# A two-layer hybrid block on one Trainium2 core: the heads' mean squares on GpSimd instead of TensorE

## The chip, the cores and the metric

The kernel runs on one core of one Trainium2 chip. The metric is the device time of one execution in microseconds (us). It was run three times: 1317.89 us in the median, 1317.74 to 1318.26. TensorE is PE in the profile (its weight loads are PEld), VectorE is DVE, ScalarE is ACT, GpSimd is POOL, SyncE is SP.

## What is computed

A sequence of 16 meta tokens and 256 tokens of width 1024 (272 columns in the kernel) passes through two layers. Each layer has a mixer of three branches (retention with 4 heads of 256 values, HGRN2 with 8 heads of 128, differential attention with 8 heads of 128) and a convolved feed-forward part. Each head's output is normalised by its own root mean square:

```python
def _rms(x):
    xf = x.astype(F32)
    return xf * lax.rsqrt(jnp.mean(xf * xf, axis=-1, keepdims=True) + EPS)
...
    o = _rms(from_chunks(o)) * jax.nn.silu(gate)        # retention
...
    o = _rms(from_chunks(o)) * jax.nn.silu(gate)        # hgrn2
...
    o = _rms(o) * subln_g.astype(F32) * (1.0 - lambda_init)   # differential attention
```

The change touches only this mean over a head's features, `jnp.mean(xf * xf, axis=-1)`.

## The kernel before

**Layout.** Activations stand transposed: features across the 128 partitions, tokens along the columns. A head of 128 features is one tile of 128 partitions by 272 columns (258 in the last layer, where only what the output needs is computed; 256, 242 or 128 in attention, whose leading and trailing tokens are treated apart). So the mean over a head's features is a sum across partitions, for each column.

**The main stream.** Every weight matrix is cut into tiles of 128 by 128, and eight tiles make a chunk of 512 KB that SP loads into `wraw` (3 buffers). ACT rounds it into `whi`, DVE subtracts to get `wlo` (4 buffers each), and PE makes three products for each tile, high by high, high by low and low by high (lines 905 to 907, in `products`). That is 11,862 products with all the small ones.

**The heads.** Between the main products PE runs the small products of the heads. `ret_head` (line 1015, four calls a layer) takes two PSUM banks of the tag `acc` for its two halves of 128 values, squares both with ACT, adds them with DVE, and multiplies both halves by the inverse root. `hg_outputs` (line 1210, two calls a layer, "a" and "b", four heads each) and `da_head` (line 1263, eight calls a layer, through `sub_norm`, line 1319) take one `acc` bank a head; `da_tail` (line 1327, two calls a layer) calls `sub_norm` once for its 128 left-over columns. The tag `acc` has two banks, so a later head's first product waits until an earlier head's `tt(y, o, r)` has read its bank. All in all there are 22 means a layer, 44 in the kernel.

**One mean** is `mean`, line 958: ACT rounds the squares into `hsh`, DVE subtracts to get `hsl`, and PE multiplies both by a matrix of 1/128 (`ones_h`) into a bank `ms`, which then holds the mean in every partition. `rsqrt` (line 804) makes two ACT passes of it, Ln with `eps` and Exp, into `hr`.

**GpSimd** has little to do: the adds and products of the layer norms (`y`, `sum`), and small copies and clears for the heads (`tails`, `wts`, `dt`, `da`, `am`, `near`, `at`).

**Order.** No engine's order is written out by hand. Each instruction is registered with a key (a due time, from a clock that counts main products) and a cost, and `_Plan.order` (line 447) simulates all five engines with those costs and deals out each engine's instructions in the order in which they would start. On the chip each engine then runs its list in that order and waits where an operand isn't ready. The costs are in `_Engine` (line 558). A changed cost or dependency anywhere can move any instruction after it.

**Memory.** The tag `slot` has 13 buffers (`SLOTS`) of 128 partitions by 1088 columns, 4352 bytes of each partition, for the blocks of the mixer. `_places` (line 142) puts the weights at chosen offsets, counted in lines of 256 bytes, against the activations that they meet.

Of the kernel before, what the change touches and what calls it, by code (L numbers as in the profile page):

```python
# [10 lines left out]

F32 = mybir.dt.float32
F32R = mybir.dt.float32r
U8 = mybir.dt.uint8
AF = mybir.ActivationFunctionType
ALU = mybir.AluOpType
PSUM = bass.MemoryType.PSUM
ADD, SUB, MUL = ALU.add, ALU.subtract, ALU.mult

P = 128  # L20
# [3 lines left out]
T = META + SEQ  # L24
# [10 lines left out]
TAIL = T - 2 * P  # L35
BANK = 512
CHUNK_TILES = 8
SLOTS = 13
LEAD = 6.0
MARGIN = 12.0  # L40
EARLY = 12.0
# [516 lines left out]
class _Engine:  # L558
# [5 lines left out]
    def __getattr__(self, method):  # L564
        f = getattr(self.engine, method)

        def call(*args, **kw):
            aps = [(k, x) for k, x in list(enumerate(args)) + list(kw.items()) if isinstance(x, bass.AP)]
            outs = [x for k, x in aps if k in (0, "out", "accum_out")]
            ins = [x for k, x in aps if k not in (0, "out", "accum_out")]  # L570
            n = math.prod(outs[0].shape[1:])
            cost = self.fixed + self.each * n
            if self.name == "act":
                cost += 0.093 * (len(aps) - 2) - (0.043 if ins[0].tensor.name in self.plan.psum else 0.0)
            elif self.name == "pool" and method != "memset":
                cost += 1.6e-3 * n
            if method == "reciprocal":
                cost += 7 * self.each * n
            elif method == "tensor_tensor_scan":
                cost += self.each * n  # L580
            elif method == "transpose":
                cost = 0.11
            elif method == "matmul" and args[1].dtype == F32R:
                cost = max(0.107, n / 2400 + 0.003)
            elif method == "matmul":
                cost = max(0.214 if args[1].shape[-1] > 32 else 0.07, 4 * n / 2400)
            elif method == "dma_start":
                cost = self.fixed + self.each * n * outs[0].shape[0]
            self.plan.add(self.name, lambda: f(*args, **kw), cost, outs, ins, args[2] if method == "activation" else None)  # L589

        return call
# [57 lines left out]
def _trace(ctx, tc, plan, a, depth, probe):  # L649
    nc = tc.nc  # L650
    act = _Engine(plan, nc.scalar, "act", 0.094, 0.833e-3)
    dve = _Engine(plan, nc.vector, "dve", 0.068, 1.042e-3)
    pe = _Engine(plan, nc.tensor, "pe", 0.0, 4 / 2400)
    pool = _Engine(plan, nc.gpsimd, "pool", 0.04, 0.85e-3)
# [7 lines left out]
    tp = ctx.enter_context(tc.tile_pool(name="tp", bufs=2))  # L662
# [6 lines left out]
    def new(pool_, shape, dt, tag, bufs, name):  # L669
        serial[0] += 1  # L670
        return plan.tile(pool_, shape, dt, tag, bufs, f"{name}_{serial[0]}")

    def fixed(shape, name, dt=F32):
        return new(cp, shape, dt, name, 1, name)

    def slot(name, dt=F32):
        return new(sp, [P, 4 * T], dt, "slot", SLOTS, name)

# [12 lines left out]
    def bank(name):  # L691
        return new(bp, [P, 512], F32, "bank", 2, name)
# [46 lines left out]
        pool.memset(t, value)  # L739
        return t  # L740

    def ones_round(value, name):
        t = fixed([P, P], name, F32R)
        f = slot("ones")[:, :P]
        pool.memset(f, value)
        act.activation(t, f, AF.Copy)
        return t

    ones_d = ones(1.0 / D, "ones_d")

    plan.key = -9.5
# [1 line left out]
    for _ in range(WARM):  # L753
        pe.matmul(warm[:, :P], ones_d, ones_d, start=True, stop=True)
    plan.key = -5.0
    ones_h = ones_round(1.0 / 128, "ones_h")
    eps = fixed([P, 1], "eps")
    pool.memset(eps, EPS)
    fmap = fixed([P, DEPTH], "fmap")
# [44 lines left out]
    def rsqrt(out, ms, scale=1.0):  # L804

        act.activation(out, ms, AF.Ln, bias=eps, scale=scale)
        act.activation(out, out, AF.Exp, scale=-0.5)

    class Norm:
# [29 lines left out]
        def mean(self):  # L839

            tt(self.acc[:, 0, :], self.acc[:, 0, :], self.acc[:, 1, :], ADD)
            self.ps = bank("ms")[:, self.first : T]
            pe.matmul(self.ps, ones_d, self.acc[:, 0, :], start=True, stop=self.rest is None)
# [111 lines left out]
        act.activation(vs, pm[:, :P], AF.Copy)  # L955
        return vs

    def mean(ones_, sq):

        n = sq.shape[1]  # L960
        hi = new(tp, [P, T], F32R, "hsh", 2, "hsh")[:, :n]
        lo = new(tp, [P, T], F32R, "hsl", 1, "hsl")[:, :n]
        act.activation(hi, sq, AF.Copy)
        dve.tensor_tensor(out=lo, in0=sq, in1=hi.bitcast(F32), op=SUB)
        ms = bank("ms")[:, :n]
        pe.matmul(ms, ones_, hi, start=True, stop=False)
        pe.matmul(ms, ones_, lo, start=False, stop=True)
        return ms

    def split_blocks(name, blocks, t0):  # L970

# [8 lines left out]
    for li in range(depth):  # L980
# [4 lines left out]
        t0 = T0 if last else 0  # L985
# [29 lines left out]
        def ret_head(hd):  # L1015
            q, k, vt, gate = st["rq"], st["rk"], st["rvt"], st["rg"]
            if hd == 0:
                st["dec"] = slot4("dec")
                sync.dma_start(st["dec"].rearrange("p h t -> p (h t)"), a["dec"])
            dec = st["dec"][:, hd, :]  # L1020

            s1 = bank("s1")
            a1 = temp(T + P + TAIL, "wts")
            parts = ((0, t0, t0, dec[:, t0:]), (P, P, T, dec[:, : P + TAIL]))
            for k0, q0, at, _ in parts:
                pe.matmul(s1[:, at : at + T - q0], k[:, hd, k0 : k0 + P], q[:, hd, q0:], start=True, stop=True)
                plan.hold(a1)
            for _, q0, at, by in parts:
                tt(a1[:, at : at + T - q0], s1[:, at : at + T - q0], by, MUL)
            os = [acc_bank("ro") for _ in range(2)]  # L1030
            sq = temp2("sum", 1)
            for e in range(2):
                o = os[e]
                ec = slice((hd * 2 + e) % 4 * P, (hd * 2 + e) % 4 * P + P)
                v = vt[(hd * 2 + e) // 4]
                pe.matmul(o[:, t0:T], v[:, 0, ec], a1[:, t0:T], start=True, stop=False)
                pe.matmul(o[:, P:T], v[:, 1, ec], a1[:, T : T + P + TAIL], start=False, stop=True)
            for e in range(2):
                i = (e * 4 + hd) * TAIL
                tt(os[e][:, 2 * P : T], os[e][:, 2 * P : T], st["ro"][:, i : i + TAIL], ADD)  # L1040
            for e in range(2):
                act.activation(sq[:, e, t0:], os[e][:, t0:T], AF.Square)
            tt(sq[:, 0, t0:], sq[:, 0, t0:], sq[:, 1, t0:], ADD)
            r = temp(T, "hr")
            rsqrt(r[:, t0:], mean(ones_h, sq[:, 0, t0:]), 0.5)
            for e in range(2):
                g = gate[:, hd * 2 + e, t0:]
                y = temp(T, "ho")[:, t0:]
                tt(y, os[e][:, t0:T], r[:, t0:], MUL)
                tt(g, y, g, MUL)  # L1050
# [159 lines left out]
        def hg_outputs(b, am, at, ax):  # L1210
            vt = st[f"hvt{b}"]
            pt = bank("ht")[:, : 4 * TAIL]
            pe.matmul(pt, st[f"hvs{b}"], am, start=True, stop=True)
            inside = temp(4 * TAIL, "am", 3)
            act.activation(inside, pt, AF.Copy)
            for hd in range(4):
                g = st["hg"][:, 4 * b + hd, t0:]
                o = acc_bank("ho")
                ec = slice(hd * P, hd * P + P)
                pe.matmul(o[:, t0:P], vt[:, 0, ec], at[:, hd, t0:P], start=True, stop=False)  # L1220
                pe.matmul(o[:, P:T], vt[:, 0, ec], ax[:, hd, :], start=False, stop=False)
                pe.matmul(o[:, P:T], vt[:, 1, ec], at[:, hd, P:], start=False, stop=True)
                tt(o[:, 2 * P : T], o[:, 2 * P : T], inside[:, hd * TAIL : (hd + 1) * TAIL], ADD)
                sq = temp(T, "hsq")
                act.activation(sq[:, t0:], o[:, t0:T], AF.Square)
                r = temp(T, "hr")
                rsqrt(r[:, t0:], mean(ones_h, sq[:, t0:]))
                y = temp(T, "ho")[:, t0:]
                tt(y, o[:, t0:T], r[:, t0:], MUL)
                tt(g, y, g, MUL)  # L1230
# [88 lines left out]
        def sub_norm(out, o):  # L1319
            n = o.shape[1]  # L1320
            sq = temp(T, "hsq")[:, :n]
            act.activation(sq, o, AF.Square)
            r = temp(T, "hr")[:, :n]
            rsqrt(r, mean(ones_h, sq))
            stt(out, o, subg[:, li : li + 1], r, MUL, MUL)

        def da_tail(b):
# [111 lines left out]
        for name, j in ORDER:  # L1439
# [18 lines left out]
            elif name[0] == "*":  # L1458
                plan.key = clock[0] - MARGIN
                n = name[1:]  # L1460
                if n == "b2":
                    blocks = [st["da0"], st["da1"]]
                else:
                    t = st["rg" if n == "b0" else "hg"]
# [6 lines left out]
            if name in BASE:  # L1471
                lo = 0 if name in FULL else t0
# [17 lines left out]
                elif name in ("dq", "dk"):  # L1490
                    t = block(f"{name}{j // 2}")
# [12 lines left out]
                elif name in ("hi", "dv"):  # L1504
                    n = name[0] + "v"
# [13 lines left out]
                else:  # L1519
                    t = block(f"{name}{j // 2}")  # L1520
# [95 lines left out]
```

## Time and profile before

| | |
|---|---|
| Median of three runs | 1317.89 us |
| The profiled execution's own time | 1318.42 us |
| Its span, first to last instruction | 1316.6 us |
| Granted TensorE clock | 0.999 |
| Busy: PE, DVE, ACT, POOL | 99%, 73%, 62%, 6% of the span |
| DMA: bytes, mean rate | 219.07 MB, 166 GB/s |

The profile is that of one execution. The execution's time is 1.8 us longer than the span. A row of a group reads: line, engine, operation, written tile <- read tiles, shape, count, then times. Instructions that go through the kernel's engine wrapper all carry line 589, so they are told apart by their tiles. PE's records overlap, because products are pipelined: what one costs PE is the distance to the next one's start, not its recorded length.

### The profile page before, as it was taken

How to read it: one execution, taken by the hardware profiler on the slowest of the kernel's cores; microseconds unless marked ns; L12 is line 12 of the kernel's file. 1: busy time of each engine (PE TensorE's matmuls, PEld its weight loads, DVE VectorE, ACT ScalarE, POOL GpSimd, SP SyncE). 2: the span in 40 equal slices, each digit the busy share in tenths (PEclk: the TensorE clock that was granted, in tenths of full speed). 3: DMA queues.
4: the chain of work that ended last, by engine and by line, in shares of the span. 5: the costliest groups of instructions: out<-in, count | busy, mean ns of one | idle time of the engine just before them, and what ended most of it. 6: DMA issues, size and time to landing. Idle time of an engine off the chain costs nothing.

```text
span 1316.6 us, 28935 instructions
## 1 busy us (share of the span) xinstructions
PE 1305.5 (99%) x11862; PEld 1278.1 (97%) x11862; DVE 962.9 (73%) x1633; ACT 816.9 (62%) x1377; POOL 83.5 (6%) x161
## 2 busy tenths in 40 slices
PE   9999999999999999999999999999999999999998
PEld 9999999999999999999999999999999999999986
DVE  7675777697576789886574757776986867898853
ACT  6847454756676567665456574557566775767643
POOL 5000000001010020000030000000011100200000
PEclk9999999999999999999999999999999999999999
DMA  7544543443534545555555445434445446465653
GB/s 274 195 148 156 169 154 129 145 145 129 186 135 161 176 160 171 185 175 183 179 175 185 161 154 167 163 131 144 144 158 171 142 159 203 144 208 191 199 189 110
DMA packets 60755, 219.07 MB, mean 166 GB/s; under 512 B 6864, under 2 KB 6992, under 8 KB 60624
## 3 DMA queue, kind: packets, MB, share of 16 engines
q1 hardware_dynamic: 60336, 216.71, 48.8%
q8 instruction: 93, 1.52, 0.5%
q10 hardware_dynamic: 288, 0.52, 0.1%
q14 instruction: 38, 0.31, 0.1%
HBM read 216.16 MB, written 1.05 MB: 165 GB/s over the span
## 4 chain that ended last, share of the span: by engine, by line
PE 96%; DVE 2%; ACT 1%; DMA 0%; issue 0%; SPq 0%; DVEq 0%
PE main L905 28%; PE main L907 27%; PE main L906 27%; PE fo L1417 2%; PE fo L1416 2%; PE fo L1415 2%; PE lev L1096 1%; PE ds L1280 1%; PE ms L589 1%; PE do L589 1%; PE ro L589 1%; PE ho L589 1%; PE vt L589 1%; DVE two_b L589 1%; DVE wlo L589 1%; PE s L589 0%
## 5 line engine op out<-in xcount | busy, mean ns | idle before, releaser
L905 PE MATMUL main<-xh,whi 128*128 128x272 f32 (+1 forms) x2368 | 689.9, 291 | 0.5 <-ACT whi L589 0.5
L906 PE MATMUL main<-xl,whi 128*128 128x272 f32 (+1 forms) x2368 | 674.1, 285 | 2.0 <-DVE xl L589 2.0
L907 PE MATMUL main<-xh,wlo 128*128 128x272 f32 (+1 forms) x2368 | 673.6, 284 | 1.0 <-DVE wlo L589 0.8
L589 DVE TENSOR_TENSOR wlo<-wraw,whi 128x1024 fp32r<-128x1024 f32 (+1 forms) x411 | 497.3, 1215 | 195.2 <-ACT whi L589 194.1
L589 ACT ACTIVATE whi<-wraw 128x1024 fp32r<-128x1024 f32 (+1 forms) x411 | 427.0, 1042 | 222.7 <-PE main L906 152.0
L906 PEld LDWEIGHTS main<-xl,whi 128*128 128x128 f32 x2368 | 446.1, 188 | 3.0 <-DVE xl L589 2.4
L907 PEld LDWEIGHTS main<-xh,wlo 128*128 128x128 f32 x2368 | 446.1, 188 | 2.5 <-DVE wlo L589 2.2
L905 PEld LDWEIGHTS main<-xh,whi 128*128 128x128 f32 x2368 | 445.9, 188 | 2.4 <-ACT whi L589 0.7
L589 DVE SCALAR_TENSOR_TENSOR two_b<-main,small,two_b 128x256 f32<-128x256 f32 (+2 forms) x144 | 65.3, 487 | 27.4 <-ACT two_b L589 25.6
L589 POOL TENSOR_TENSOR y<-h,rstd 128x272 f32<-128x272 f32 x32 | 34.6, 1115 | 314.4 <-ACT rstd L589 314.4
L589 ACT ACTIVATE two_b<-main,small 128x272 f32<-128x272 f32 (+1 forms) x72 | 37.3, 566 | 25.6 <-PE main L907 25.6
L905 PE MATMUL main<-ghi,whi 128*128 128x272 f32 x176 | 51.0, 290 | 0.0
L906 PE MATMUL main<-glo,whi 128*128 128x272 f32 x176 | 50.6, 287 | 0.0
L907 PE MATMUL main<-ghi,wlo 128*128 128x272 f32 x176 | 50.3, 286 | 0.0
L589 ACT ACTIVATE vsrc<-main 128x544 f32<-128x544 f32 x24 | 15.0, 626 | 38.5 <-PE main L907 38.3
L905 PE MATMUL main<-b0hi,whi 128*128 128x272 f32 (+1 forms) x128 | 38.1, 298 | 0.0
L905 PE MATMUL main<-b1hi,whi 128*128 128x272 f32 (+1 forms) x128 | 38.0, 297 | 0.0
L905 PE MATMUL main<-yhi,whi 128*128 128x272 f32 (+1 forms) x128 | 36.4, 284 | 0.0
L906 PE MATMUL main<-b0lo,whi 128*128 128x272 f32 (+1 forms) x128 | 36.4, 284 | 0.0
L906 PE MATMUL main<-b1lo,whi 128*128 128x272 f32 (+1 forms) x128 | 36.4, 284 | 0.0
L907 PE MATMUL main<-b0hi,wlo 128*128 128x272 f32 (+1 forms) x128 | 36.4, 284 | 0.0
L907 PE MATMUL main<-b1hi,wlo 128*128 128x272 f32 (+1 forms) x128 | 36.4, 284 | 0.0
(244 smaller groups left out, 1933.4 us busy)
## 6 DMA issues: line engine op xcount, KB each, us to landing
wraw<-in_w SPq DMA_DIRECT2D x402, 512.0 KB, 3.3
h<-in_h SPq DMA_DIRECT2D x4, 272.0 KB, 5.1
dec<-in_dec SPq DMA_DIRECT2D x2, 544.0 KB, 5.6
wraw<-in_w SPq DMA_DIRECT2D x4, 256.0 KB, 4.5
const<-in_const SPq DMA_DIRECT2D x1, 937.0 KB, 5.4
gain<-in_gl SPq DMA_DIRECT2D x1, 512.0 KB, 5.0
out<-y ACTq DMA_DIRECT2D x2, 256.0 KB, 2.8
out<-y SPq DMA_DIRECT2D x2, 256.0 KB, 2.7
```

What stands on the lines that cost most here:

```text
L589: self.plan.add(self.name, lambda: f(*args, **kw), cost, outs, ins, args[2] if method == "activation" else None)
L905: nc.tensor.matmul(o, wh, hi, start=first, stop=False)
L906: nc.tensor.matmul(o, wh, lo, start=False, stop=False)
L907: nc.tensor.matmul(o, wl, hi, start=False, stop=last)
L1096: nc.tensor.matmul(o, keys, x, start=True, stop=True)
L1280: nc.tensor.matmul(ss[m][:, at : at + nk], q[half, hd, q0 : q0 + P], k[half, hd, :nk], start=True, stop=True)
L1415: nc.tensor.matmul(o, gh, wh, start=False, stop=False)
L1416: nc.tensor.matmul(o, gl, wh, start=False, stop=False)
L1417: nc.tensor.matmul(o, gh, wl, start=False, stop=end)
```

## The change

`mean` is gone with its two tiles and with `ones_h`; `inverse` takes its place. GpSimd's `partition_all_reduce` adds the squares over all 128 partitions in fp32 and writes the sum to every partition of `r`; the Ln pass then takes the factor 1/n as its scale (n is 256 in retention, 128 elsewhere), and still adds `eps`. The planner gets a cost for the new operation, and `SLOTS` goes from 13 to 14.

```diff
+from concourse.bass_isa import ReduceOp
...
-SLOTS = 13
+SLOTS = 14
...
+            if method == "partition_all_reduce":
+                cost = 0.4 + 5.4e-3 * n
...
-    def ones_round(value, name):
-        t = fixed([P, P], name, F32R)
-        f = slot("ones")[:, :P]
-        pool.memset(f, value)
-        act.activation(t, f, AF.Copy)
-        return t
...
-    ones_h = ones_round(1.0 / 128, "ones_h")
...
-    def mean(ones_, sq):
-
-        n = sq.shape[1]
-        hi = new(tp, [P, T], F32R, "hsh", 2, "hsh")[:, :n]
-        lo = new(tp, [P, T], F32R, "hsl", 1, "hsl")[:, :n]
-        act.activation(hi, sq, AF.Copy)
-        dve.tensor_tensor(out=lo, in0=sq, in1=hi.bitcast(F32), op=SUB)
-        ms = bank("ms")[:, :n]
-        pe.matmul(ms, ones_, hi, start=True, stop=False)
-        pe.matmul(ms, ones_, lo, start=False, stop=True)
-        return ms
+    def inverse(r, sq, n):
+
+        pool.partition_all_reduce(r, sq, P, ReduceOp.add)
+        rsqrt(r, r, 1.0 / n)
...
-            rsqrt(r[:, t0:], mean(ones_h, sq[:, 0, t0:]), 0.5)
+            inverse(r[:, t0:], sq[:, 0, t0:], 2 * P)
...
-                rsqrt(r[:, t0:], mean(ones_h, sq[:, t0:]))
+                inverse(r[:, t0:], sq[:, t0:], P)
...
-            rsqrt(r, mean(ones_h, sq))
+            inverse(r, sq, P)
```

## The prediction, made before the result was known

> **What bounds the kernel now.** I read the page's busy row first, then its chain, then what PE waited for.
>
> ```profile
> span 1316.6 us, 28935 instructions
> PE 1305.5 (99%) x11862; PEld 1278.1 (97%) x11862; DVE 962.9 (73%) x1633; ACT 816.9 (62%) x1377; POOL 83.5 (6%) x161
> PE 96%; DVE 2%; ACT 1%; DMA 0%; issue 0%; SPq 0%; DVEq 0%
> ```
>
> PE is busy for 99% of the span and makes 96% of the chain that ends last. A busy PE could still be stretched by waits, so the second view is who PE waited for in the whole kernel:
>
> ```profile
> PE main L906 <- DVE xl L589: 2.0, 2, 1.6
> PE warm L589 <- POOL ones_d L589: 1.0, 1, 1.0
> PE main L907 <- DVE wlo L589: 0.8, 3, 0.3
> PE main L905 <- ACT whi L589: 0.5, 1, 0.5
> PE wt L589 <- DVE two_a L589: 0.2, 1, 0.2
> ```
>
> These are 4.5 us in all, and none is a wait for a head. PE runs through, so a product that leaves PE's list shortens the kernel by the distance it took, unless a new wait fills the hole.
>
> The third view is PE's order in time around one mean, first at 272 columns and then at 128:
>
> ```profile
> 115.42 0.28 PE L906 MATMUL main<-xl,whi 128*128 128x272 f32 x1
> 115.54 0.29 PE L907 MATMUL main<-xh,wlo 128*128 128x272 f32 x1
> 115.67 0.29 PE L589 MATMUL ms<-hsh,ones_h 128*128 128x272 f32 x1
> 115.80 0.28 PE L905 MATMUL main<-xh,whi 128*128 128x272 f32 x1
> ...
> 331.85 0.23 PE L589 MATMUL ms<-hsh,ones_h 128*128 128x128 f32 x1
> 331.92 0.34 PE L905 MATMUL main<-xh,whi 128*128 128x272 f32 x1
> ```
>
> The recorded 0.29 us overlaps its neighbours. What the product takes from PE is 115.80 - 115.67 = 0.13 us, and 0.07 us at 128 columns.
>
> **The change, part by part.** What leaves:
>
> ```profile
> L589 PE MATMUL ms<-hsh,ones_h x44: 223/284/379, 115.7 to 1064.2; 128*128 128x272 f32 x12, 128*128 128x258 f32 x12, 128*128 128x256 f32 x8, 128*128 128x242 f32 x8
> L589 PE MATMUL ms<-hsl,ones_h x44: 224/284/359, 117.3 to 1065.4; 128*128 128x272 f32 x12, 128*128 128x258 f32 x12, 128*128 128x256 f32 x8, 128*128 128x242 f32 x8
> L589 ACT ACTIVATE hsh<-hsq x36: 310/417/443, 114.7 to 1063.3; 128x272 fp32r<-128x272 f32 x8, 128x256 fp32r<-128x256 f32 x8, 128x258 fp32r<-128x258 f32 x8, 128x242 fp32r<-128x242 f32 x8
> L589 ACT ACTIVATE hr<-ms,eps x44: 347/475/491, 118.9 to 1066.3; 128x272 f32<-128x272 f32 x12, 128x258 f32<-128x258 f32 x12, 128x256 f32<-128x256 f32 x8, 128x242 f32<-128x242 f32 x8
> L589 DVE TENSOR_TENSOR hsl<-hsq,hsh x36: 277/420/443, 115.5 to 1064.2; 128x272 fp32r<-128x272 f32 x8, 128x256 fp32r<-128x256 f32 x8, 128x258 fp32r<-128x258 f32 x8, 128x242 fp32r<-128x242 f32 x8
> ```
>
> *PE, on the path.* 88 products go: 24 each at 272 and 258 columns, 16 each at 256 and 242, and the 8 left over at 128. On the line between 0.07 us at 128 and 0.13 us at 272 the middle ones take 0.124, 0.123 and 0.118 us. The sum is 24 x 0.13 + 24 x 0.124 + 16 x 0.123 + 16 x 0.118 + 8 x 0.07 = **10.5 us**.
>
> *ACT and DVE, beside PE.* The 44 roundings at 0.417 us are 18.3 us of ACT, the 44 subtractions at 0.42 us are 18.5 us of DVE. Both engines stand beside a PE that is never out of work, so I cost this gain at nothing. The same holds for the clear and the copy that made `ones_h`, and for the fourteenth slot: more room can only start something earlier, and PE waits for no slot. It takes 4352 bytes; the tiles that leave free 3 x 1088 + 512 bytes. 512 and 4352 are both whole lines of 256 bytes, so the offsets of weights against activations stay as they are, and I cost the shift at nothing too.
>
> *POOL, what is added.* 44 reductions, 22 in each layer. The trace has none. Nearest are POOL's own passes over a tile of this size:
>
> ```profile
> L589 POOL TENSOR_TENSOR y<-h,rstd x32: 767/972/1779, 21.1 to 1137.3; 128x272 f32<-128x272 f32 x32
> L589 POOL COPY dt<-two_a x32: 197/198/1132, 294.1 to 1057.4; 128x16 f32<-128x16 f32 x32
> L589 POOLq MODIFY_POOL_CONFIG  x2: 13/13/13, 1.1 to 1.1; - x2
> L589 POOL TENSOR_TENSOR y<-h,rstd 128x272 f32<-128x272 f32 x32 | 34.6, 1115 | 314.4 <-ACT rstd L589 314.4
> ```
>
> From below: one pass, 0.77 us, since every element must be read once. From above: a sum of 128 partitions made pairwise takes seven steps, seven passes at the mean of 1.115 us, 7.8 us. I take two passes, one to collect and one to hand the sum back to all partitions, 2.2 us, because a pass is the row that it is nearest to and the result has to travel both ways. The planner's own figure in the diff, 0.4 + 0.0054 x 272 = 1.87 us, is what the order is made with; it proves nothing about the chip. In all POOL gets about 44 x 2.2 = 97 us of work beside its 83.5 us, far from full.
>
> *The chain of one head.* In the view of tiles the first rounding starts at 114.7 us and the first Ln at 118.9: 4.2 us. The last pair of rows gives 1063.3 and 1066.3: 3.0 us. The new link is a hop, the reduction and a hop. So at 2.2 us it is not longer than what it replaces, as long as POOL has one head at a time. It doesn't in group b of `hg_outputs`, whose heads come in pairs:
>
> ```profile
> 259.55 0.69 ACT L589 ACTIVATE hsq<-ho 128x272 f32<-128x272 f32 x2
> 262.09 0.49 ACT L589 ACTIVATE hr<-ms,eps 128x272 f32<-128x272 f32 x1
> 262.61 0.43 ACT L589 ACTIVATE hr<-hr 128x272 f32<-128x272 f32 x1
> 265.16 0.42 DVE L589 TENSOR_TENSOR ho<-ho,hr 128x272 f32<-128x272 f32 x1
> 266.44 0.38 PE L589 MATMUL ho<-at,vt 128*128 128x128 f32 x2
> ```
>
> The second of a pair has its squares at 259.55 + 0.69 = 260.24, its bank is free at 265.16 + 0.42 = 265.58, and PE wants that bank at 266.44. So 6.2 us may pass. The new way takes two reductions in a row, Ln 0.49, Exp 0.43, the product 0.42 and three hops of about 0.1: 2R + 1.64. It fits up to R = 2.3 us. Beyond that PE itself stands still, with all main products queued behind the head's. Four pairs (two in each layer) lose 2 us for each us more, and the eight retention heads, which each hold both `acc` banks, lose 1 us: some 16 us for each us of R over 2.3.
>
> R can be stretched by VectorE. The copy of 16 columns above takes 0.198 us at the median and 1.132 at most, and the 272-column product goes from 0.767 to 1.779: POOL at times waits almost for one whole DVE instruction, such as this one:
>
> ```profile
> L589 DVE TENSOR_TENSOR wlo<-wraw,whi x411: 420/1223/1798, 5.8 to 1300.2; 128x1024 fp32r<-128x1024 f32 x132, 128x512 fp32r<-128x512 f32 x4, 128x256 fp32r<-128x256 f32 x1
> ```
>
> If one reduction in four of a pair meets it in full, the mean R is 2.2 + 0.25 = 2.45, and the loss is (2.45 - 2.3) x 16 = 2.4 us. Between nothing (no meeting, or the new order spaces the heads) and 2.4 us I take **1 us**.
>
> [...] By the longest `wlo`, 1798 against 1223 ns, DVE is held too; what that would make of the time is the second rival.
>
> *What waits behind.* POOL's list is in order: a copy of `tails`, `wts` or `dt` behind a reduction waits for that head's squares. ACT's list is too: the Ln stands before roundings of `whi`. Four buffers of eight tiles at 3 x 0.125 us are 12 us of lead, more than any R that I expect, so I cost both at nothing; without that lead each us would be PE's.
>
> *The sum.* 1318.42 - 10.5 + 1.0 = 1308.9 us against the profiled execution. That one stands 0.5 us above the median of 1317.89, so against the median it is **1308.4 us**.
>
> **The rivals.**
>
> *The code for the reduction has to be loaded (1316 us).* Two MODIFY_POOL_CONFIG stand just ahead of the first tensor product on POOL and none later. If the reduction lives in other code than tensor products, POOL must switch four times: before each layer's first head, and back before the products `y` that follow the heads.
>
> ```profile
> 9.48 1.36 POOL L589 TENSOR_TENSOR sum<-sum,two_c 128x544 f32<-128x544 f32 x1 [8.36 <-ACT two_c L589]
> 100.61 0.15 POOL L589 MEMSET tails<- 128x64 f32 x1
> 761.69 0.15 POOL L589 MEMSET tails<- 128x64 f32 x1
> 480.11 8.47 POOL L589 TENSOR_TENSOR y<-h,rstd 128x272 f32<-128x272 f32 x8 [63.15 <-ACT rstd L589]
> ```
>
> One load takes at most the 8.36 us that POOL was idle at the start, and ACT ended even that idle time. Before the first squares (114.7 us) POOL has nothing after 100.8 us, in the second layer nothing between 761.8 and the squares near 773 us, and before `y` it idles 63 us. So all four are hidden in this order. If the new order exposes one, PE loses about 8.4 - 0.9 (266.44 - 265.58) = 7.5 us: 1308.4 + 7.5 = 1316. [...]
>
> *DVE becomes the bound where heads are thick (1314 us).*
>
> ```profile
> 260.00:280.00 20.00, 20.00 (x164) 20.00 (x163) 17.99 (x33) 12.27 (x22) 0.00 (x0) 1.00 0.42 136
> 280.00:300.00 20.00, 20.00 (x161) 19.20 (x160) 17.00 (x46) 10.88 (x31) 0.72 (x4) 1.00 0.48 159
> 300.00:320.00 20.00, 20.00 (x159) 19.12 (x159) 15.28 (x43) 11.47 (x31) 2.93 (x6) 1.00 0.46 154
> 320.00:340.00 20.00, 20.00 (x164) 19.92 (x163) 16.09 (x30) 13.53 (x32) 1.18 (x6) 1.00 0.41 135
> ```
>
> The fourth number of a row is DVE's busy time: 66.4 of 80 us. Nine heads fall in here (four of group b, four of attention, one tail). If each reduction held DVE for its full 2.2 us, that is 66.4 + 9 x 2.2 - 9 x 0.42 = 82.4 us: 2.4 us too much here and as much in the second layer, 1308.4 + 5 = 1314. Against it: even the longest `wlo` is only 0.58 us over its median.
>
> *The reduction is slow, and POOL sets the pace of the heads (1344 us, slower than before).* The place is the pairs and the retention heads above; the price is 16 us for each us of R over 2.3. The gain is used up at R = 2.3 + 9.5/16 = 2.9 us: from there the change loses. At four passes, 4.5 us, it is 1308.4 + 2.2 x 16 = 1344; at seven, 1308.4 + 5.5 x 16 = 1396. For it: a sum across partitions has no row here, and 2.9 is not far over 2.2. Against it: the order is replanned around the new operation, and the chain's hops are dearer in the planner (0.4 us) than the tenths between rows. [...]
>
> *It changes nothing (1318 us).* The products go, and the new order finds 10 us of other waits. For it: any instruction may move. Against it: today's order leaves PE only 4.5 us of waits over 1300.
>
> **How the numbers follow.** A time within 0.2% of before, 1315.3 to 1320.5 us, can't be told from no change. The forecast (1305 to 1312) has 0.75, a DVE bound 0.06, an exposed load 0.05, no change 0.03, a slow reduction 0.11, of which 0.01 is the very slow one. The forecast reaches down to 1305 if most of the 4.5 us of PE's waits fall out of the new order, and up to 1312 if the loss is 2.4 us and the waits double. The range goes on over the DVE case and the load to 1317; the slow reduction is left out. Faster: the forecast, the DVE case and a load at the page's price, 0.83. Same: most of the load, no change, 0.05. Slower: the slow reduction and two exposed loads, 0.12.
>
> **What would show it.** Right: 88 fewer PE instructions; PE busy near 1295 us and still 99%; a POOL group of 44 with `hr` as output at 2 to 2.5 us; ACT's `hr` waiting for POOL in place of PE; DVE and ACT each 18 us less; PE's waits under 8 us with no head's `ho`, `ro` or `do` among them. Wrong: reductions over 2.9 us with PE waiting for `ho` or `ro`; MODIFY_POOL_CONFIG with a long POOL idle time behind it that a head's Ln waits out; `wlo` well over 1.3 us at the mean and PE waiting for `wlo`.

## The result, and the profile after

| | before | after |
|---|---|---|
| Median | 1318.41 us (6 runs, 1317.74 to 1319.05) | 1309.12 us (6 runs, 1308.46 to 1310.34) |
| Ratio to before | | 0.9931, 95% interval 0.9918 to 0.9943 |
| Span of the profiled execution | 1316.6 us | 1307.8 us |
| PE instructions | 11,862 | 11,774 |

The change makes the kernel faster by 9.3 us, 0.7%. The forecast was 1308.4 us with a range of 1305 to 1317. The page of the changed kernel, its busy row and its chain by engine:

```profile
span 1307.8 us, 28691 instructions
PE 1295.4 (99%) x11774; PEld 1266.6 (97%) x11774; DVE 959.0 (73%) x1589; ACT 801.6 (61%) x1332; POOL 169.8 (13%) x204
PE 92%; DVE 5%; ACT 1%; DMA 1%; issue 1%; SPq 0%; POOL 0%; DVEq 0%; ACTq 0%
```

PE's busy time fell by 10.1 us and its share stayed at 99%. The chain went from 96% PE and 2% DVE to 92% and 5%: PE is still the bound, but DVE has a larger part in the chain. Who PE waited for, in the changed kernel:

```profile
PE main L901 <- DVE xl L592: 2.0, 2, 1.7
PE warm L592 <- POOL eps L592: 1.0, 1, 1.0
PE main L902 <- DVE wlo L592: 1.0, 4, 0.3
PE ds L592 <- DVE dk L592: 0.7, 1, 0.7
PE wt L592 <- DVE two_a L592: 0.6, 3, 0.3
PE main L900 <- ACT whi L592: 0.4, 1, 0.4
PE do L592 <- DVE tw L592: 0.3, 1, 0.3
PE wt L592 <- POOL dt L592: 0.2, 1, 0.2
```

These are 6.2 us against 4.5 before. The first three rows and the sixth stood in the old kernel with nearly the same numbers. What came is waits of `ds`, `wt` and `do` (`wt` had 0.2 us before): small products of attention whose operands come late by tenths of a microsecond. None is for `ho` or `ro`, where the prediction had looked for them first; `do`, which it also wanted free of waits, has 0.3 us.

The reductions in the changed kernel, by the tile `hr` (min, median and max in ns):

```profile
L592 POOL PARTITION_ALL_REDUCE hr<-hsq x36: 1078/1872/2877, 115.5 to 1056.3; - x36
L592 POOL PARTITION_ALL_REDUCE hr<-sum x8: 1850/1867/1887, 217.1 to 899.0; - x8
```

POOL's configurations, which the prediction named as the sign of a load of code, in the view of its line:

```profile
L592 POOLq MODIFY_POOL_CONFIG  x10: 10/11/11, 1.1 to 1059.5; - x10
```

A reduction of 272 columns takes 1.87 us, one of 128 columns 1.08 at the least. The longest are stretched to 2.9 us. The two pool configurations of before are ten now, five pairs: one at the start as before (1.1 us), and four (101.4, 411.9, 758.2 and 1059.5 us) at switches between tensor products and reductions, where the prediction had placed them. That code is loaded there is the author's reading: the views show the pairs, and the idle time that can go with one. Copies and clears stand between the reductions too, and none of them brought a pair: none falls between 101.4 and 411.9 us or between 758.2 and 1059.5.

```profile
101.12 0.31 POOL L592 MEMSET near<- 128x256 f32 x1 [18.57 <-ACT at L592]
115.53 2.60 POOL L592 PARTITION_ALL_REDUCE hr<-hsq  x1 [14.10 <-ACT hsq L592]
...
411.43 0.41 POOL L592 COPY da<-tw 128x64 f32<-128x64 f32 x2 [1.54 <-DVE tw L592]
476.33 8.47 POOL L592 TENSOR_TENSOR y<-h,rstd 128x272 f32<-128x272 f32 x8 [64.49 <-ACT rstd L592]
...
757.65 0.31 POOL L592 MEMSET near<- 128x256 f32 x1 [17.92 <-ACT at L592]
769.14 1.87 POOL L592 PARTITION_ALL_REDUCE hr<-hsq  x1 [11.18 <-ACT hsq L592]
...
1122.84 8.63 POOL L592 TENSOR_TENSOR y<-h,rstd 128x272 f32<-128x272 f32 x8 [63.37 <-ACT rstd L592]
```

In this timeline of POOL (start, length, what; in brackets the idle time and what ended it) each switch falls into an idle time of 11 us or more that data ends: ACT's squares or the layer norm, not a load.

### The profile page after: what moved, and what is told of

It is laid out like the page before. It is cut to its first block, busy times and chain, and to the rows that moved or that the text cites. A ratio compares the mean times of both kernels' runs of the same rounds, so it can differ in the third digit from the quotient of the medians.

```text
span 1307.8 us, 28691 instructions
## 1 busy us (share of the span) xinstructions
PE 1295.4 (99%) x11774; PEld 1266.6 (97%) x11774; DVE 959.0 (73%) x1589; ACT 801.6 (61%) x1332; POOL 169.8 (13%) x204
## 4 chain that ended last, share of the span: by engine, by line
PE 92%; DVE 5%; ACT 1%; DMA 1%; issue 1%; SPq 0%; POOL 0%; DVEq 0%; ACTq 0%
PE main L900 27%; PE main L902 26%; PE main L901 26%; PE fo L1403 2%; PE fo L1404 2%; PE fo L1405 2%; DVE wlo L592 1%; PE lev L1084 1%; DVE two_b L592 1%; PE ds L1268 1%; PE ro L592 1%; PE ho L592 1%; PE vt L592 1%; DVE two_a L592 1%; PE do L592 1%
## 5 line engine op out<-in xcount | busy, mean ns | idle before, releaser
L592 DVE TENSOR_TENSOR wlo<-wraw,whi 128x1024 fp32r<-128x1024 f32 (+1 forms) x411 | 503.4, 1230 | 186.9 <-ACT whi L592 185.9
L592 POOL PARTITION_ALL_REDUCE hr<-hsq x36 | 72.0, 2016 | 120.9 <-ACT hsq L592 120.9
L592 POOL COPY tails<-vsrc 128x32 f32<-128x32 f32 x32 | 11.8, 383 | 224.6 <-ACT vsrc L592 224.6
L902 PE MATMUL main<-yhi,wlo 128*128 128x272 f32 (+1 forms) x128 | 36.4, 284 | 0.0
```

The lines of the kernel that those rows point to most:

```text
L902: nc.tensor.matmul(o, wl, hi, start=False, stop=last)
```

## The experiments

Ten kernels were run, in three groups. Each group has its own runs of the kernel before, so ratios are given against those; times in one group compare directly. The change itself ran again in the first group only, so runs of the other two are set beside it, or beside 13 slots, by their ratios.

| run | median, us | ratio to before, interval |
|---|---|---|
| *first group, before* | 1317.97 | |
| the change again | 1308.93 | 0.9927 (0.9914 to 0.9939) |
| 13 slots | 1308.56 | 0.9925 (0.9913 to 0.9938) |
| 13 slots, split kept | 1310.99 | 0.9944 (0.9932 to 0.9957) |
| 13 slots, split and products kept | 1322.04 | 1.0025 (1.0016 to 1.0035) |
| *second group, before* | 1318.04 | |
| two reductions a head | 1319.54 | 1.0009 (0.9999 to 1.0018) |
| planner's price 0.01 us | 1319.79 | 1.0013 (1.0004 to 1.0022) |
| planner's price 0.5 us higher | 1308.83 | 0.9927 (0.9912 to 0.9942) |
| loads between the reductions | 1351.23 | 1.0250 (1.0234 to 1.0265) |
| *third group, before* | 1318.48 | |
| before, with reductions unread | 1319.17 | 1.0006 (0.9997 to 1.0015) |
| 13 slots, products alone kept | 1319.32 | 1.0005 (0.9996 to 1.0014) |

The ratio goes by all the runs, near their means, and the table by medians. In the first group the runs of the kernel before spread upward, from 1317.24 to 1321.37 us, so that times set against it come out 0.4 to 0.8 us lower by the ratio than by the medians.

**The change again**, as the reference of its group, unaltered.

> The changed kernel once more, with nothing altered, as the reference for the other three on the same chip. Expected: 1309.1 us, 0.993 of before. If it lands over 0.3% away from that, differences of 2 us between the others can't be read.

It gave 1308.93 us, so the group can be read.

**13 slots.**

```diff
-SLOTS = 14
+SLOTS = 13
```

> The changed kernel with 13 slots in place of 14. Theory (the gain is the time of 88 products on PE, and nothing else): the same within 1 us, 1309 us, since PE waits for no slot. Rival (the fourteenth slot carries part of the gain): 1311 us or more, with waits of PE that were not there.

1308.56 us (1308.24 to 1309.28 over its runs, against 1308.28 to 1309.69 with 14): the fourteenth slot is worth nothing that can be measured, as the theory had it.

**The split kept, unread.**

```diff
-SLOTS = 14
+SLOTS = 13
...
     def inverse(r, sq, n):
 
+        m = sq.shape[1]
+        hi = new(tp, [P, T], F32R, "hsh", 2, "hsh")[:, :m]
+        lo = new(tp, [P, T], F32R, "hsl", 1, "hsl")[:, :m]
+        act.activation(hi, sq, AF.Copy)
+        dve.tensor_tensor(out=lo, in0=sq, in1=hi.bitcast(F32), op=SUB)
         pool.partition_all_reduce(r, sq, P, ReduceOp.add)
```

> 13 slots, and each head still rounds its squares on ACT and subtracts on DVE as before the change, though nothing reads the two tiles; only the 88 products are gone. Theory: 18 us of work on ACT and 18 us on DVE lie beside PE, so 1309 us, the same as with 13 slots alone within 1.5 us. Rival (relief of ACT and DVE is where the gain comes from): 1314 us or more, half of the gain lost or all.

1310.99 us, 2.4 us more than 13 slots alone, and the runs of the two don't overlap (1309.97 to 1312.23 against 1308.24 to 1309.28). Neither number of the expectation was met: beside the reductions the split is not free, and it isn't where most of the gain comes from. Where it costs is in PE's waits of that run:

```profile
PE ds L592 <- DVE dk L592: 2.6, 2, 1.7
...
PE vm L592 <- POOL tails L592: 0.9, 1, 0.9
```

The wait for `dk`, 0.7 us in the changed kernel, is 2.6 us here, and 0.9 us of waiting for `tails` is new. `dk` is a rotation by DVE between the HGRN2 heads and attention, where DVE is busy for 19.83 of 20 us in the changed kernel.

The kept subtraction isn't what it was in the kernel before, though. It reads the same squares as the reduction, at about the same time:

```profile
L592 DVE TENSOR_TENSOR hsl<-hsq,hsh x36: 280/610/1405, 114.6 to 1058.0; 128x272 fp32r<-128x272 f32 x8, 128x256 fp32r<-128x256 f32 x8, 128x258 fp32r<-128x258 f32 x8, 128x242 fp32r<-128x242 f32 x8
```

It takes 0.61 us at the median and 1.41 at most, against 0.42 and 0.44 in the prediction's row. So the 2.4 us are the price of a split beside reductions; what the split cost without them, this run doesn't show.

**Split and products kept, unread.**

```diff
...
+    ones_h = ones_round(1.0 / 128, "ones_h")
...
         dve.tensor_tensor(out=lo, in0=sq, in1=hi.bitcast(F32), op=SUB)
+        ms = bank("ms")[:, :m]
+        pe.matmul(ms, ones_h, hi, start=True, stop=False)
+        pe.matmul(ms, ones_h, lo, start=False, stop=True)
         pool.partition_all_reduce(r, sq, P, ReduceOp.add)
```

> As the run with the split kept, and PE also makes the 88 products with ones into a bank that nothing reads; the reduction on GpSimd still gives the result. Theory: 10.5 us more than with the split alone, 1319 to 1320 us, a little over the kernel before because the reductions' own cost of 1 to 2 us stays. Rival (the gain came from the shorter chain of a head, the freed bank of PSUM or the relief of ACT and DVE): under 1314 us.

1322.04 us, 2 us over the theory and far from the rival: the 88 products cost 1322.04 - 1310.99 = 11.05 us. PE has its 11,862 instructions back. And with everything of the old kernel kept, the reductions put 4.1 us on top of it (3.3 us by the ratio). Part of that is the meeting of reduction and subtraction, which now keeps PE waiting:

```profile
PE ms L592 <- DVE hsl L592: 1.8, 4, 0.8
L592 DVE TENSOR_TENSOR hsl<-hsq,hsh x36: 279/702/1407, 114.7 to 1069.4; 128x272 fp32r<-128x272 f32 x8, 128x256 fp32r<-128x256 f32 x8, 128x258 fp32r<-128x258 f32 x8, 128x242 fp32r<-128x242 f32 x8
```

**Products alone kept.** The same 88 products, on a tile of the layer norm's activations, with no split.

```diff
-        hi = new(tp, [P, T], F32R, "hsh", 2, "hsh")[:, :m]
-        lo = new(tp, [P, T], F32R, "hsl", 1, "hsl")[:, :m]
-        act.activation(hi, sq, AF.Copy)
-        dve.tensor_tensor(out=lo, in0=sq, in1=hi.bitcast(F32), op=SUB)
+        x = x_tile(0, False)[0][:, :m]
         ms = bank("ms")[:, :m]
-        pe.matmul(ms, ones_h, hi, start=True, stop=False)
-        pe.matmul(ms, ones_h, lo, start=False, stop=True)
+        pe.matmul(ms, ones_h, x, start=True, stop=False)
+        pe.matmul(ms, ones_h, x, start=False, stop=True)
```

> The changed kernel with 13 slots and, for each head, 88 products in all of the same size into a bank that nothing reads, but on a tile that is there anyway, so ACT and DVE do no split. Theory (the products cost PE 11 us by themselves and the split costs 2.4 us by itself): 1308.6 + 11 = 1319.6 us, 2.4 us under the run with both. Rival (the split's 2.4 us came from something that the two have in common, such as a later bank): as the run with both, 1322 us. Second rival (the products cost so much only because they wait for the split): 1316 us or less.

1319.32 us, as the theory had it. By the ratios the products cost (1.0005 - 0.9925) x 1318 = 10.5 us over 13 slots alone, and the split another (1.0025 - 1.0005) x 1318 = 2.6 us. Both ways round, the two parts have the same sizes; beside the reductions they add, and the products don't need the split to be dear. The same run gives what the kernel gets for exchanging the split for the reductions: against the kernel before, which has the same products, it is 0.0005 x 1318 = 0.7 us longer, with no change inside the interval.

**Before, with reductions that nobody reads.** The kernel before, whole, and a reduction in place after each split, with the planner's price for it from the change; the squares' tile is held until it is done.

```diff
...
         pe.matmul(ms, ones_, hi, start=True, stop=False)
         pe.matmul(ms, ones_, lo, start=False, stop=True)
+        pool.partition_all_reduce(sq, sq, P, ReduceOp.add)
         return ms
```

> The kernel before the change, with its split, its products and 13 slots, and besides that GpSimd reduces each head's squares in place once the split has read them; nothing reads the result, so no head waits for a reduction. The run with split and products kept, where the heads do wait for it, was 4.1 us over before. Theory (these 4 us are the heads' longer chain and its place in the order of the engines): within 1 us of before, 1317 to 1319 us. Rival (a reduction hurts by holding DVE up, whoever reads it): 1320 us or more, 3 us or more over before.

1319.17 us, 0.8 us over its own before by the ratio, with no change inside the interval. That is a little above the 1317 to 1319 of the first line and under the rival's 1320. So reductions that no head waits for cost little. They do hold DVE up: the same 1633 instructions keep it busy for 973.1 us in place of 962.9, 0.23 us more for each reduction.

Against the run with split and products kept, the ratios differ by (1.0025 - 1.0006) x 1318 = 2.5 us. That heads wait for the reduction there is one explanation. It isn't the only one: here the reduction stands behind the subtraction, which is back at its old median, and PE waits 0.5 us for `hsl` in place of 1.8.

```profile
L592 DVE TENSOR_TENSOR hsl<-hsq,hsh x36: 279/422/1405, 114.5 to 1066.8; 128x272 fp32r<-128x272 f32 x8, 128x256 fp32r<-128x256 f32 x8, 128x258 fp32r<-128x258 f32 x8, 128x242 fp32r<-128x242 f32 x8
```

And the instructions of the two kernels stand in another order. These runs don't separate the three.

**Two reductions a head.** The second reduces the first one's result; the scale takes the factor 128 out.

```diff
         pool.partition_all_reduce(r, sq, P, ReduceOp.add)
-        rsqrt(r, r, 1.0 / n)
+        pool.partition_all_reduce(r, r, P, ReduceOp.add)
+        rsqrt(r, r, 1.0 / (n * P))
```

> Each head reduces twice in a row: the squares, then the result once more, and the scale takes the factor 128 out again. The planner prices both. A head's chain grows by one reduction, 1.9 us, to R = 3.9 us. By the prediction's rule (16 us lost for each us of R over 2.3): 1309 + 1.6 x 16 = 1335 us, with PE waiting for ho and ro. Rival (the planner knows the price and spaces the heads, so PE finds other products): 1309 to 1312 us.

1319.54 us, (1.0009 - 0.9927) x 1318 = 10.8 us more for 1.87 us more in each chain: 5.8 us lost for each us of R. Neither expectation fits. The planner knows the price and still PE waits, 15.1 us in all against 6.2 in the changed kernel. But the loss is less than half of the 25.6 us that the rule gave, and most of it is elsewhere:

```profile
PE wt L592 <- DVE wts L592: 3.2, 2, 1.6
PE wt L592 <- DVE two_a L592: 2.9, 6, 1.3
...
PE ds L592 <- DVE dk L592: 1.8, 1, 1.8
PE ho L592 <- DVE ho L592: 1.3, 1, 1.3
```

All four are heads' work in which DVE is late; only the last, 1.3 us, is a product that waits for an `acc` bank, and none is `ro`.

**The planner's price at nothing.**

```diff
-                cost = 0.4 + 5.4e-3 * n
+                cost = 0.01
```

> The planner takes the reduction to cost 0.01 us; the instructions are the same, only their order may differ. Theory (the order keeps PE fed, and the planner's price is what makes the order fit): the heads' next products come 1.9 us too early in PE's list, 16 places lose up to 1 us each, 1312 to 1325 us. Rival (hops priced at 0.4 us and a PE that runs slower than planned leave slack enough): within 1 us of 1309 us.

1319.79 us: the same instructions, dealt out in another order, lose 11 us, more than the change had won. The number lies in the theory's 1312 to 1325. How it comes about is to be seen on DVE and PE in the second half of that kernel's first mixer:

```profile
271.51 0.78 DVE L592 STREAM_SHUFFLE two_c<-main 128x544 f32<-128x544 f32 x1
272.19 0.70 DVE L592 TENSOR_TENSOR dk<-main,const 128x544 f32<-128x544 f32 x1
274.70 0.79 DVE L592 TENSOR_TENSOR ho<-ho,hr 128x272 f32<-128x272 f32 x2 [1.81 <-ACT hr L592]
275.52 0.79 DVE L592 TENSOR_TENSOR hg<-ho,hg 128x272 f32<-128x272 f32 x2
276.23 0.72 DVE L592 TENSOR_TENSOR two_c<-two_c,const 128x544 f32<-128x544 f32 x1
276.99 0.72 DVE L592 TENSOR_TENSOR dk<-dk,two_c 128x544 f32<-128x544 f32 x1
```

```profile
275.65 0.28 PE L902 MATMUL main<-xh,wlo 128*128 128x272 f32 x1
277.76 0.43 PE L592 MATMUL ds<-dk,wts 128*128 128x64 f32 x2 [1.82 <-DVE dk L592]
```

The planner, told that a reduction is free, put the heads' `ho` ahead of the last two steps of the rotation `dk`. On the chip `hr` isn't there yet: DVE stands still for 1.81 us in the middle of a rotation whose operands are ready, `dk` comes late, and PE stops for 1.82 us with its main products queued behind `ds`. Here a late reduction reaches PE through what is behind it in DVE's list. PE's waits for `ds` are the largest of that kernel with 3.4 us, and its waits for `ho`, which the theory had in mind, 1.4 us. All its listed waits are 11.7 us against 6.2, so this view places half of the 11 us; the other half isn't located.

**The planner's price 0.5 us higher.**

```diff
-                cost = 0.4 + 5.4e-3 * n
+                cost = 0.9 + 5.4e-3 * n
```

> The planner's price is 0.5 us higher, 2.37 us at 272 columns, which covers a reduction that waits for DVE. Theory (the 1.7 us that the change gave back are waits of PE for reductions that came late by a few tenths): 1308 us, with PE's waits for ds, wt and do gone. Rival (these waits belong to the new order and not to the price): 1309 us or up to 2 us either way.

1308.83 us against 1308.93. In that profile PE's waits for `ds` and `do` are gone, those of `wt` have grown, and the sum is 4.6 us against 6.2. The median is the same all the same: it can't tell the theory's 1308 from the rival's 1309. The optimum is flat on this side, and this is no better version than the change.

**Loads between the reductions.** A tensor product of one element between the squares and the reduction of each retention head.

```diff
+            pool.tensor_tensor(out=r[:, t0 : t0 + 1], in0=sq[:, 0, t0 : t0 + 1], in1=sq[:, 0, t0 : t0 + 1], op=ADD)
             inverse(r[:, t0:], sq[:, 0, t0:], 2 * P)
```

> In each retention head POOL first adds one column of squares to itself, an element that the reduction then overwrites: a tensor product between two reductions, so that other code must be loaded before it and the reduction's after it, 8 times; the planner knows nothing of a load. Theory (a load takes 5 to 8.4 us and is hidden in the changed kernel only because POOL has idle time of 10 us and more where it switches): MODIFY_POOL_CONFIG before each of these, PE waiting for ro, 1309 + 8 x (6 to 7.5 - 0.9 or so), 1340 to 1362 us. Rival (the load is cheap, or runs beside the work): under 1315 us.

1351.23 us, (1.0250 - 0.9927) x 1318 = 42.6 us more, 5.3 us a head, inside the theory's range. POOL's timeline at the first of them:

```profile
216.61 0.19 POOL L592 TENSOR_TENSOR hr<-sum 128x1 f32<-128x1 f32 x1 [22.17 <-DVE sum L592]
222.61 1.90 POOL L592 PARTITION_ALL_REDUCE hr<-sum  x1 [5.81 <-issue]
```

All its loads, in the view of the line:

```profile
L592 POOLq MODIFY_POOL_CONFIG  x42: 1/11/98, 1.1 to 1100.8; - x42
```

PE's largest wait in that kernel:

```profile
PE ro L592 <- DVE ho L592: 22.9, 6, 6.0
```

Between the end of the tensor product at 216.80 and the reduction at 222.61 POOL waits for nothing that the profile shows: 5.8 us, the price of one load here. At a later head, before the reduction at 926.12, it is 6.79 us. With it in a head's chain the `acc` banks do become free too late, and PE waits for `ro`, as the prediction had it for a slow reduction. The 32 more configurations are 16 pairs, two in each of eight heads.

## Why the prediction held, step by step

The first group gives the change in its parts, from before to after:

| step | us | running |
|---|---|---|
| before | | 1317.97 |
| reductions put in, everything else kept | +4.07 | 1322.04 |
| 88 products out | -11.05 | 1310.99 |
| split out | -2.43 | 1308.56 |
| slot 14 | +0.37 | 1308.93 |

These are differences of medians, and each belongs to its place in the row: all three kernels between have reductions in them.

- **The products.** 10.5 us was the term; 11.05 us in the first group, 10.5 by the ratios on another tile. The reading that set it was the distance between starts (0.13 us), not the recorded length (0.28 us). This is the cause of the gain, and the step that carried the forecast.
- **ACT and DVE beside PE, at nothing.** Beside the reductions the split costs 2.4 us, so there nothing was too little. PE's old 4.5 us of waits had been taken as proof that these engines have room everywhere. Over the whole kernel they have (DVE 73% and ACT 62% busy); where a group of heads, a rotation and the weights' split meet, DVE hasn't. In the changed kernel that stretch reads (PE, weight loads, DVE, ACT, POOL):

```profile
260.00:280.00 20.00, 19.29 (x157) 19.08 (x156) 19.83 (x34) 9.61 (x16) 6.99 (x4) 1.00 0.40 135
```

  DVE is busy for 19.83 of 20 us, against 17.99 between the same times before, and it is here that PE misses 0.71 us, its wait for `dk`. Room has to be read in the thick stretch, not from the share of the span. What the split cost in the old kernel, where no reduction met it, is not shown.
- **The slot, at nothing.** Right: 0.4 us, within the spread of both runs. The working finds 512 and 4352 bytes to be whole lines of 256 and passes over the 3 x 1088 of the two tiles, which are 12.75 lines. But main products take 0.28 to 0.29 us at the mean in both kernels, so if anything shifted, it cost nothing that shows.
- **The reduction's length.** 2.2 us from two passes, 1.87 us measured, 2.0 in the mean of the 36 that read `hsq`. Stretched ones reach 2.9, as the rows of copies had warned.
- **The cost of the reductions, 1 us.** As a net of reductions put in and split taken out it fits: 4.07 - 2.43 = 1.6 us by the medians of the first group, 0.7 us by the ratio of the run with products alone kept. Singly the two are 4.1 (3.3 by the ratio) and 2.4 us beside each other, where reduction and subtraction meet. If they are as large apart, the prediction mis-sized two terms with opposite signs and was lucky; if not, it had both about right. No run has neither split nor reductions, so this stays open. Of the 0.7 us by which the total is off, 0.5 is the median of before, 1318.41 in six runs against 1317.89 in three; as a change, 9.5 us were forecast and 9.3 measured.
- **The place and the rule of 16 us for each us.** The failed step, though the forecast stood only 1 us on it. Pairs of heads and the retention heads were to wait for `acc` banks. In the changed kernel no `ho` or `ro` waits; doubling the reduction loses 10.8 us where the rule gives 25.6, with only 1.3 us of PE's waits at `ho`; only a delay of 5.8 us that the planner doesn't know brings `ro` to a stop. The slack had been read from the old order (0.86 us at one pair), but the planner deals out a new one around the price that it is given. The run with the price at nothing shows how much hangs on that.
- **What waits behind, at nothing.** Incomplete. The prediction looked at POOL's and ACT's lists and at `whi`; it didn't ask what stands behind `ho` on DVE, which needs the late `hr`. In the run with the price at nothing that is how a late reduction stops PE.
- **The loads.** Four switches, at the foretold places, each hidden; where one isn't, POOL stood idle for 5.8 us at one head and 6.79 at another. No trace ahead of that run shows what a load in the open takes, neither the 6 us in its expectation nor the price at which the chance of "faster" counts one in: before had only the 8.36 us of idle time. No row or run shows the very slow reduction that has a chance of 0.01 either; this operation takes 1.87 us at 272 columns.
- **DVE as the bound.** DVE is held up. In the changed kernel, at the pair of reductions that POOL runs from 264.93 for 5.22 us:

```profile
264.93 5.22 POOL L592 PARTITION_ALL_REDUCE hr<-hsq  x2 [3.16 <-ACT hsq L592]
...
264.95 0.71 DVE L592 TENSOR_TENSOR two_c<-two_c,const 128x544 f32<-128x544 f32 x1
265.70 1.57 DVE L592 TENSOR_TENSOR dk<-dk,two_c 128x544 f32<-128x544 f32 x1
267.19 3.32 DVE L592 TENSOR_TENSOR wlo<-wraw,whi 128x1024 fp32r<-128x1024 f32 x2
```

  The second rotation product takes 1.57 us where others of its shape take 0.72, two `wlo` take 3.32 in place of about 2.4, and the two reductions 5.22 in place of 3.74: each holds the other. In the kernel before, no `dk` product took over 0.73 us. These holds, 1.7 us in all, stand just ahead of PE's wait for the next `dk`, so they may have made it; no run shows that alone.

  But the reduction doesn't keep DVE out for its whole length: the `two_c` above took 0.71 us inside a reduction, as it did in the kernel before. Over the kernel DVE's busy time fell by 3.9 us and not by the 18 that the prediction expected (ACT's by 15.3). So some 14 us came back as longer instructions, a third of a microsecond for each reduction where the second rival had 2.2; in the run with unread reductions it is 0.23 us, and the time there is 0.8 us longer, with no change inside the interval.
- **Slips in the working.** 1308.4 + 5 is 1313.4 us for the second rival, not 1314, and a loss of 2.4 us with doubled waits gives 1308.4 + 1.4 + 4.5 = 1314.3 us, not 1312. The result hangs on neither.

What stays open: how the 4.1 us divide between waiting heads, held-up DVE (the kept subtraction first of all) and mere difference of order. The runs give bounds, not a clean division, since every edit makes the planner deal out a new order.

## What to carry to other kernels

With PE busy for 99% of the span, work taken off it paid its full start-to-start distance here (88 products, 10.5 to 11.05 us), and a slower operation on an idle engine could take it over; with the chain longer by one reduction, 1.87 us, the gain was gone. A new operation also needs a true price in whatever decides the order: an engine's list is run as dealt, and one instruction that waits for a late operand holds back ready work behind it (DVE for 1.81 us and then PE for 1.82, in the run with the price at nothing). Work that is kept, unread, in an experiment can meet the new work (the kept subtraction took 0.61 us in place of 0.42), so its price there isn't its price in the old kernel. Count switches between kinds of GpSimd operations, and look for an idle time longer than a load, 5.8 to 6.79 us here, at each.

## What the runs showed of the hardware

In the run with loads between the reductions, PE's stops had a second price. The stretches of that kernel (PE busy first, then weight loads, DVE, ACT, POOL, granted clock, DMA):

```profile
200.00:220.00 20.00, 20.00 (x157) 19.68 (x156) 15.07 (x28) 7.08 (x10) 0.19 (x1) 1.00 0.40 133
220.00:240.00 20.00, 12.68 (x83) 11.88 (x81) 5.37 (x12) 4.99 (x9) 3.98 (x3) 0.91 0.24 79
240.00:260.00 20.00, 15.91 (x87) 14.83 (x88) 9.05 (x17) 9.11 (x14) 2.08 (x2) 0.77 0.23 77
260.00:280.00 20.00, 18.07 (x129) 17.71 (x128) 9.90 (x16) 13.05 (x23) 4.10 (x7) 0.89 0.34 111
280.00:300.00 20.00, 20.00 (x165) 20.00 (x164) 17.43 (x31) 11.06 (x19) 9.20 (x5) 1.00 0.41 133
```

The granted clock fell to 0.77 in the stretch from 240 to 260 us, where PE got through 87 instructions; the stretch ahead of the stops had 1.00 and 157. In the changed kernel it stays at 1.00 through the same stage. What that makes of a product is in PE's timeline of that kernel just after one stop, with the stretch of 2 us around its last three rows:

```profile
241.24 3.11 PE L592 MATMUL ro<-wts,rvt 128*128 128x272 f32 x8 [4.37 <-DVE ho L592]
...
244.61 0.43 PE L902 MATMUL main<-xh,wlo 128*128 128x272 f32 x1
244.83 0.43 PE L900 MATMUL main<-xh,whi 128*128 128x272 f32 x1
245.06 0.43 PE L901 MATMUL main<-xl,whi 128*128 128x272 f32 x1
...
244.00:246.00 2.00, 2.00 (x11) 2.00 (x11) 0.62 (x2) 0.65 (x2) 0.00 (x0) 0.50 0.74 262
```

After 4.37 us of standing still the granted clock is 0.50, and main products start 0.225 us apart, against the 0.12 of the rows in the prediction. So the stops of this run cost more than themselves: the waits for `ro` and `ho` are 22.9 and 3.5 us there, and the kernel lost 42.6. The mean granted clock of that execution was 0.986, against 0.999 before; an estimate from these two, 0.013 x 1349 = 17.5 us, is about the size of the other 16 us. The prediction's slow rival, priced by stops alone, left this out.
